# The taps of a depthwise convolution in another rhythm, with a later rank

## The chip, the cores and the metric

One NeuronCore of a Trainium2 chip runs the whole program. The metric is the device time of one execution in microseconds (us); less is better. Engines: TensorE (PE in the rows, its weight loads PEld), VectorE (DVE), ScalarE (ACT), GpSimd (POOL), and SyncE (SP), which issues the DMAs.

## What is computed

Two layers of a decoder trunk on 512 tokens of width 1024, in fp32. Each layer is a gated feed-forward half step, a token mixer, and a second feed-forward half step. The change lies in the mixer:

```python
def conv_module(u, conv_w, conv_b, ln_g, ln_b):
    u1, u2 = jnp.split(u, 2, axis=-1)
    u = u1 * jax.nn.sigmoid(u2)
    y = lax.conv_general_dilated(u, conv_w[:, None, :].astype(u.dtype), window_strides=(1,),
                                 padding=[(CONV_K - 1, 0)],
                                 dimension_numbers=('NWC', 'WIO', 'NWC'),
                                 feature_group_count=u.shape[-1]) + conv_b
    return jax.nn.silu(layernorm(y, ln_g, ln_b))

def token_mixer(...):
    proj = h @ w_in
...
    y_a = dilated_mixer(qa, ka, va, rel_bias[:, :HA]).reshape(b, s, A_W)
...
    ob = diff_attention(qb, kb, vb, lam, rel_bias[:, HA:])
    y_b = (rmsnorm(ob, subln_g) * (1.0 - lam_init)).reshape(b, s, B_W)
    y_c = conv_module(u, conv_w, conv_b, conv_ln_g, conv_ln_b)
    ys = jnp.einsum('gbsm,gmd->bsgd', jnp.stack([y_a, y_b, y_c]), w_branch)
    gates = jax.nn.sigmoid(h @ w_gate + b_gate).reshape(b, s, N_BRANCH, d)
    return jnp.sum(gates * ys, axis=2) @ w_out
```

The convolution has 31 taps and 512 channels, each channel for itself.

## The kernel before

Activations lie transposed, channels on partitions and the 512 tokens along the free dimension. Every fp32 weight and activation is split into a high and a low part (`halves`, lines 221 to 231: the high part by ScalarE in L226, the low part by VectorE in L230; `split`, L268 and L269, for activations), and each product is three matmuls (L274, L276, L278; in the projections L832, L834, L836). Weights come by DMA from SyncE into five raw buffers (`raw`, L218) and wait as split pairs in three.

The mixer (L1080) first makes the four channel tiles `u` of the convolution's input (`conv_in`, L719). Then it interleaves three streams that are written out by hand:

- the *filler*: the matmuls of the q, k, v projections for seven of eight heads' blocks (`project`, L816, 96 matmuls each; block 0 runs before), and then the first branch's gates (`gates`, L1074, 8 x 36 matmuls);
- the *attention* of eight blocks (`attention`, L908): four of the first kind (dilated, two heads each), four of the second (differential). It calls `pull(n)` between its own instructions, which emits n matmuls of the filler;
- the *convolution* (`conv`, L751): a generator. Each `yield n` asks to be called again n ticks later; `tick` (L1094) counts one for each pulled matmul and, beyond the attention, one for each matmul of the rest of the filler and of the second branch's gates.

One tap (L770; the first of each channel tile is L768) is a VectorE instruction over 128 x 512: `ca[j] = u * w + ca[j]`. There are 4 x 31 = 124 per layer. Before, the first 93 ask for 4 ticks each and the last 31 for 14. After the last tap comes the chain of the layer norm: sums over the channels by TensorE (`token_sum`, L322), broadcasts (`token_bcast`, L331), four subtractions (L787), squares, a reciprocal root, four products (L803), and four tiles of swish and split (L810, L811, L269). It asks for 127 ticks together. The four accumulators `ca` lie in two of the five raw weight buffers until the chain is through.

In ticks: 70 are pulled before the attention, the four blocks of the first kind pull 96 each (up to tick 454), the four of the second kind 108 each (up to 886), 18 follow, the filler ends at 960, and the second gates run to 1248. The third gates need the convolution's result and run after it, without ticks.

The order on each engine is fixed at build time: a scheduler gives each engine, whenever it takes it to be free, the ready instruction of the smallest rank. The rank is the order in which the program emits instructions. On the chip each engine then runs its list in that order. So a tap can run ahead of its place when its engine has nothing else that is ready, and a tap whose place has passed goes ahead of everything emitted later.

Other lines that are named below: L841 and L842 copy v out of the projection's PSUM banks and split it, L855 to L861 normalise q and k, L902 to L928 are the softmax, L937 transposes its result, L964 and L979 multiply it by v, L1058 to L1063 apply a gate.

Of the kernel before, what the change touches and what calls it, by code (L numbers as in the profile page):

```python
# [31 lines left out]
TAPS = 31  # L32
# [41 lines left out]
class Trunk:  # L74
# [676 lines left out]
    def conv(self, l):  # L751


        nc = self.nc

        ca = []
        for _ in range(2):
            t = self.raw()
            ca += [t[:, 0:T], t[:, T:2 * T]]


        prod = self.acc

        def tap(j, i):
            w = self.p(l, PO_CONVW + j * TAPS + i)
            u = self.up[j][:, i:i + T]
            if i == 0:
                nc.vector.tensor_scalar(ca[j], u, w, self.p(l, PO_CONVB + j), op0=ALU.mult, op1=ALU.add)  # L768
            else:
                nc.vector.scalar_tensor_tensor(ca[j], u, w, ca[j], op0=ALU.mult, op1=ALU.add)  # L770


        for j in range(4):
            for i in range(TAPS):
                tap(j, i)
                yield 4 if j < 3 else 14
        toks = range(4)
        nc.vector.tensor_tensor(prod, ca[2], ca[3], op=ALU.add)
        for j in range(2):
            nc.vector.tensor_tensor(prod, prod, ca[j], op=ALU.add)  # L780
        yield 1
        mean = self.token_sum([prod], toks, 1.0 / 512, 0.0)
        yield 16
        pb = self.token_bcast(mean, toks)
        yield 4
        for j in range(4):
            nc.vector.tensor_tensor(ca[j], ca[j], pb, op=ALU.subtract)  # L787
        yield 16
        for j in range(4):
            sq = self.t2k("sq")  # L790
            nc.scalar.activation(sq, ca[j], AF.Square)
            if j == 0:
                total = sq
            else:
                nc.vector.tensor_tensor(prod if j < 3 else total, total if j == 1 else prod, sq, op=ALU.add)
            yield 10
        v = self.token_sum([total], toks, 1.0 / 512, EPS)
        r = self.rsqrt(v, 4)
        yield 32
        pb = self.token_bcast(r, toks)  # L800
        yield 1
        for j in range(4):
            nc.vector.tensor_tensor(ca[j], ca[j], pb, op=ALU.mult)  # L803
        yield 17
        self.yc = []
        for j in range(4):
            g, b = self.p(l, PO_LNG + j), self.p(l, PO_LNB + j)
            sg = self.t2k("sg")
            nc.scalar.activation(sg, ca[j], AF.Sigmoid, bias=b, scale=g)
            nc.vector.tensor_scalar(ca[j], ca[j], g, b, op0=ALU.mult, op1=ALU.add)  # L810
            nc.vector.tensor_tensor(ca[j], ca[j], sg, op=ALU.mult)  # L811
            a = self.act_pair("yc")
            self.split(a, ca[j])
            self.yc.append(a)
# [265 lines left out]
    def mixer(self, l, stats, nxt):  # L1080
# [13 lines left out]
        def tick():  # L1094
            pull.count += 1
            if pull.count >= pull.due:
                pull.due = pull.count + next(conv, 1 << 30)
# [147 lines left out]
```

## Time and profile before

| | us |
|---|---|
| median of 3 runs | 2591.58 (2588.98 to 2593.63) |
| profiled execution | 2593.34 |
| its span | 2591.2 |
| TensorE busy | 2505.5 (97%) |
| VectorE busy | 1968.4 (76%) |
| ScalarE busy | 1124.6 (43%) |
| DMA queues, share of 16 engines | 37% |

Busy time is the time in which an engine has an instruction running. A matmul's end is modelled, so a busy TensorE need not be at its peak; the granted clock (PEclk, 1.00 is full speed, 2.4 GHz; 0.50 is 1.2 GHz) tells how fast it was allowed to run. Idle time of an engine is put down to the instruction whose end released the next one.

### The profile page before, as it was taken

How to read it: one execution, taken by the hardware profiler on the slowest of the kernel's cores; microseconds unless marked ns; L12 is line 12 of the kernel's file. 1: busy time of each engine (PE TensorE's matmuls, PEld its weight loads, DVE VectorE, ACT ScalarE, POOL GpSimd, SP SyncE). 2: the span in 40 equal slices, each digit the busy share in tenths (PEclk: the TensorE clock that was granted, in tenths of full speed). 3: DMA queues.
4: the chain of work that ended last, by engine and by line, in shares of the span. 5: the costliest groups of instructions: out<-in, count | busy, mean ns of one | idle time of the engine just before them, and what ended most of it. 6: DMA issues, size and time to landing. Idle time of an engine off the chain costs nothing.

```text
span 2591.2 us, 37974 instructions
## 1 busy us (share of the span) xinstructions
PE 2505.5 (97%) x15072; PEld 2201.5 (85%) x15072; DVE 1968.4 (76%) x3519; ACT 1124.6 (43%) x1765; POOL 30.5 (1%) x33
## 2 busy tenths in 40 slices
PE   6899999989999999999989999999899999999999
PEld 4889898877778889898989898898787778898988
DVE  8988876989873468979678796679898744785855
ACT  4435343545562345343455353435455523552533
POOL 2000000000000000000000000000000000000000
PEclk9999999989999999999999999999899999999999
DMA  7474644212223323737324553331122232233332
GB/s 264 163 244 158 236 149 127 80 46 76 78 90 98 90 74 98 260 107 260 107 65 157 209 183 123 96 88 54 50 81 78 90 94 93 66 106 98 101 97 89
DMA packets 97747, 312.20 MB, mean 120 GB/s; under 512 B 10345, under 2 KB 17257, under 8 KB 97570
## 3 DMA queue, kind: packets, MB, share of 16 engines
q1 hardware_dynamic: 97424, 309.65, 37.1%
q8 instruction: 118, 1.93, 0.3%
q14 instruction: 59, 0.48, 0.1%
q10 hardware_dynamic: 146, 0.14, 0.0%
HBM read 307.62 MB, written 6.06 MB: 121 GB/s over the span
## 4 chain that ended last, share of the span: by engine, by line
PE 82%; DVE 12%; ACT 3%; issue 2%; DMA 1%; SPq 0%; DVEq 0%; ACTq 0%
PE mm L583 16%; PE mm L274 13%; PE mm L276 13%; PE mm L278 13%; PE s L583 12%; PE mm L834 3%; PE mm L832 3%; PE mm L836 3%; DVE wr L770 2%; PE s L895 2%; DVE wl L230 2%; DVE ada L431 1%; DMA ada<-in_w_ada 1%; PE o L964 1%; DVE hx L491 1%
## 5 line engine op out<-in xcount | busy, mean ns | idle before, releaser
L226 ACT ACTIVATE wh<-wr 128x1024 fp32r<-128x1024 f32 (+1 forms) x481 | 485.2, 1010 | 641.6 <-PE mm L278 303.0
L230 DVE TENSOR_TENSOR wl<-wr,wh 128x1024 fp32r<-128x1024 f32 (+1 forms) x468 | 544.7, 1166 | 238.3 <-ACT wh L226 237.1
L274 PE MATMUL mm<-ah,wh 128*128 128x512 f32 (+1 forms) x752 | 287.1, 383 | 0.0
L274 PE MATMUL mm<-hh,wh 128*128 128x512 f32 (+1 forms) x776 | 281.6, 366 | 5.7 <-ACT wh L226 2.9
L278 PE MATMUL mm<-al,wh 128*128 128x512 f32 (+1 forms) x752 | 286.7, 382 | 0.0
L276 PE MATMUL mm<-hh,wl 128*128 128x512 f32 (+1 forms) x776 | 281.5, 366 | 5.2 <-DVE wl L230 5.2
L276 PE MATMUL mm<-ah,wl 128*128 128x512 f32 (+1 forms) x752 | 286.4, 382 | 0.0
L583 PE MATMUL mm<-sh,wh 128*128 128x256 f32 x936 | 268.4, 287 | 16.6 <-ACT wh L226 13.9
L278 PE MATMUL mm<-hl,wh 128*128 128x512 f32 (+1 forms) x776 | 276.5, 367 | 7.2 <-DVE hl L500 7.1
L583 PE MATMUL mm<-sh,wl 128*128 128x256 f32 x936 | 268.0, 286 | 0.5 <-DVE wl L230 0.5
L583 PE MATMUL mm<-sl,wh 128*128 128x256 f32 x936 | 267.7, 286 | 0.0
L509 DVE SCALAR_TENSOR_TENSOR x<-mm,res,x 128x512 f32<-128x512 f32 (+1 forms) x124 | 86.2, 697 | 156.2 <-PE mm L278 156.0
L583 PEld LDWEIGHTS mm<-sh,wh 128*128 128x128 f32 x936 | 182.1, 195 | 18.6 <-ACT wh L226 14.7
L834 PE MATMUL mm<-wl,hh 128*128 128x384 f32 x512 | 183.8, 359 | 8.5 <-DVE wl L230 8.5
L832 PE MATMUL mm<-wh,hh 128*128 128x384 f32 x512 | 177.3, 360 | 8.7 <-DVE v L842 8.7
L583 PEld LDWEIGHTS mm<-sh,wl 128*128 128x128 f32 x936 | 182.5, 195 | 1.2 <-DVE wl L230 0.8
L836 PE MATMUL mm<-wh,hl 128*128 128x384 f32 x512 | 183.5, 358 | 0.0
L583 PEld LDWEIGHTS mm<-sl,wh 128*128 128x128 f32 x936 | 182.6, 195 | 0.0
L770 DVE SCALAR_TENSOR_TENSOR wr<-u,par,wr 128x512 f32<-128x512 f32 x240 | 176.1, 744 | 0.2
L431 DVE SCALAR_TENSOR_TENSOR ada<-ada,cb 128x1024 f32<-128x1024 f32 x144 | 173.1, 1219 | 3.1 <-DMA ada<-in_w_ada 2.9
L274 PEld LDWEIGHTS mm<-hh,wh 128*128 128x128 f32 x776 | 147.6, 191 | 32.5 <-ACT hh L493 4.1
L583 PE MATMUL s<-hl,wh 128*128 128x256 f32 x624 | 175.1, 281 | 0.0
(218 smaller groups left out, 5603.8 us busy)
## 6 DMA issues: line engine op xcount, KB each, us to landing
wr<-in_w_up SPq DMA_DIRECT2D x156, 512.0 KB, 3.7
ada<-in_w_ada SPq DMA_DIRECT2D x144, 512.0 KB, 5.7
wr<-in_w_down SPq DMA_DIRECT2D x64, 512.0 KB, 5.4
wr<-in_w_qkv SPq DMA_DIRECT2D x64, 384.0 KB, 3.2
wr<-in_w_gate SPq DMA_DIRECT2D x48, 512.0 KB, 3.7
wr<-in_w_down SPq DMA_DIRECT2D x32, 384.0 KB, 3.1
wr<-in_w_branch SPq DMA_DIRECT2D x24, 512.0 KB, 3.6
wr<-in_w_u SPq DMA_DIRECT2D x16, 512.0 KB, 3.6
```

Source lines behind the costliest of these rows:

```text
L226: nc.scalar.activation(hi[:, :n], raw[:, :n], AF.Copy)
L230: eng.tensor_tensor(lo[:, :n], raw[:, :n], hi[:, :n].bitcast(F32), op=ALU.subtract)
L274: nc.tensor.matmul(ps[:, rng], w[0][:, wcol], ah[:, rng], start=start, stop=False)
L276: nc.tensor.matmul(ps[:, rng], w[1][:, wcol], ah[:, rng], start=False, stop=False)
L278: nc.tensor.matmul(ps[:, rng], w[0][:, wcol], al[:, rng], start=False, stop=stop)
L431: nc.vector.scalar_tensor_tensor(w, w, 1.0, cb, op0=ALU.mult, op1=ALU.mult, accum_out=self.mod[l][:, e:e + 1])
L509: self.nc.vector.scalar_tensor_tensor(self.x[d][:, rng], ps[:, rng], self.res[l][:, 8 * s + d:8 * s + d + 1], self.x[d][:, rng], op0=ALU.m ...
L583: nc.tensor.matmul(o, w[a][:, c], acts[k][b], start=first and (mi, k, x) == (0, 0, 0), stop=(k, x) == (3, 2), skip_group_check=True)
L770: nc.vector.scalar_tensor_tensor(ca[j], u, w, ca[j], op0=ALU.mult, op1=ALU.add)
L832: nc.tensor.matmul(o, hi[:, hs], w[0][:, ws], start=k == 0, stop=False)
L834: nc.tensor.matmul(o, hi[:, hs], w[1][:, ws], start=False, stop=False)
L836: nc.tensor.matmul(o, lo[:, hs], w[0][:, ws], start=False, stop=k == KD - 1)
```

## The change

Of each layer's 124 taps, the first 82 now ask for 5 and 6 ticks in turn, the next 24 for 18 each, and the last 18 for 8 each: 451, 432 and 144 ticks. In ticks, the three groups end at 451, 883 and 1027; before, the taps ended at 806. Each tap is also emitted with a rank 60 greater than its place (an offset of -60 in a block that otherwise makes ranks smaller), so 60 instructions emitted after it count as older. What follows the taps is as before.

```diff
-        for j in range(4):
-            for i in range(TAPS):
-                tap(j, i)
-                yield 4 if j < 3 else 14
+
+        for n in range(4 * TAPS):
+            with self.tc.high_priority(offset=-60):
+                tap(n // TAPS, n % TAPS)
+            yield 5 + n % 2 if n < 82 else 18 if n < 106 else 8
```

## Rows read from the trace of the kernel before

**Rows 1.** The page: busy time of two engines; granted clock in 40 slices.
```profile
PE 2505.5 (97%) x15072; PEld 2201.5 (85%) x15072; DVE 1968.4 (76%) x3519; ACT 1124.6 (43%) x1765; POOL 30.5 (1%) x33
...
PEclk9999999989999999999999999999899999999999
```

**Rows 2.** Windows, mixer: stretch, length, busy PE, PEld, DVE, ACT, POOL (instructions), clock, DMA.
```profile
476.00:614.00 138.00, 124.76 (x653) 102.73 (x653) 126.32 (x366) 66.88 (x183) 0.00 (x0) 0.94 0.18 52
...
614.00:767.00 153.00, 151.54 (x793) 121.09 (x792) 131.89 (x380) 88.62 (x171) 0.00 (x0) 1.00 0.26 79
767.00:834.00 67.00, 66.61 (x287) 52.99 (x286) 28.08 (x45) 20.76 (x25) 0.00 (x0) 1.00 0.35 109
...
1756.00:1896.00 140.00, 126.76 (x655) 104.69 (x656) 126.63 (x368) 67.12 (x183) 0.00 (x0) 0.93 0.18 53
...
476.00:520.00 44.00, 42.68 (x238) 35.12 (x237) 41.52 (x141) 25.49 (x70) 0.00 (x0) 1.00 0.19 60
...
614.00:680.00 66.00, 65.99 (x369) 55.62 (x368) 62.27 (x198) 34.24 (x83) 0.00 (x0) 1.00 0.31 92
```

**Rows 3.** Windows of TensorE alone: stretch, length, busy (instructions), clock, DMA.
```profile
544.00:546.00 2.00, 0.20 (x1) 0.56 0.47 91
546.00:554.00 8.00, 8.00 (x25) 0.50 0.25 94
...
568.00:572.00 4.00, 3.46 (x14) 0.57 0.34 98
```

**Rows 4.** Timeline of TensorE: start, duration, instruction, idle before it and its releaser.
```profile
568.54 0.69 PE L834 MATMUL mm<-wl,hh 128*128 128x384 f32 x1 [1.59 <-DVE wl L230]
...
587.69 0.42 PE L832 MATMUL mm<-wh,hh 128*128 128x384 f32 x1 [2.50 <-DVE v L842]
```

**Rows 5.** Timeline of VectorE before the last of these waits ended.
```profile
584.87 0.95 DVE L230 TENSOR_TENSOR wl<-wr,wh 128x768 fp32r<-128x768 f32 x1
585.74 0.74 DVE L770 SCALAR_TENSOR_TENSOR wr<-u,par,wr 128x512 f32<-128x512 f32 x1
586.40 0.28 DVE L841 CAST v<-mm 128x128 fp32r<-128x128 f32 x1
586.60 0.74 DVE L770 SCALAR_TENSOR_TENSOR wr<-u,par,wr 128x512 f32<-128x512 f32 x1
587.26 0.28 DVE L842 TENSOR_TENSOR v<-mm,v 128x128 fp32r<-128x128 f32 x1
```

**Rows 6.** Windows of line 832 alone: stretch, length, PE busy (count), PEld.
```profile
430.00:476.00 46.00, 20.51 (x61) 11.47 (x61) 1.00 0.31 90
476.00:520.00 44.00, 16.20 (x48) 8.97 (x48) 1.00 0.19 60
520.00:614.00 94.00, 26.39 (x77) 15.83 (x76) 0.91 0.17 49
```

**Rows 7.** Windows of line 770 (the taps) alone: stretch, length, DVE busy (count).
```profile
430.00:476.00 46.00, 21.86 (x31) 1.00 0.31 90
476.00:520.00 44.00, 13.39 (x18) 1.00 0.19 60
...
520.00:614.00 94.00, 34.17 (x46) 0.91 0.17 49
```

**Rows 8.** The page: DMA issues of gate weights.
```profile
wr<-in_w_gate SPq DMA_DIRECT2D x48, 512.0 KB, 3.7
```

**Rows 9.** Waits of TensorE, 476 to 614 us: total, times, longest.
```profile
PE mm L832 <- DVE v L842: 4.3, 2, 2.5
PE mm L834 <- DVE wl L230: 4.3, 4, 1.6
```

**Rows 10.** Timeline of VectorE: the first layer's last tap and pieces of the chain.
```profile
689.92 0.75 DVE L770 SCALAR_TENSOR_TENSOR wr<-u,par,wr 128x512 f32<-128x512 f32 x1
...
721.69 2.48 DVE L787 TENSOR_TENSOR wr<-wr,s 128x512 f32<-128x512 f32 x4 [0.89 <-PE s L331]
...
768.07 0.69 DVE L269 TENSOR_TENSOR ycl<-wr,ych 128x512 fp32r<-128x512 f32 x1 [0.30 <-ACT ych L268]
```

## The prediction

> **What bounds the kernel now.** I read the page first. TensorE is busy for 97% of the span and VectorE for 76%, and the granted clock is near full speed: of the 40 slices of 64.8 us only the ninth (from 518 us) and the 29th (from 1814 us) show a lower one, one in each layer's mixer [rows 1]. So most of the kernel is TensorE's own work, and a change of VectorE's order can win only where TensorE waits. All idle TensorE time together is 2591.2 - 2505.5 = 85.7 us.
>
> Then I cut the mixer of the first layer into stretches [rows 2]. The reader is to see that it changes its limit. In the 138 us of the first four heads (476 to 614) TensorE is busy for 124.8 us at a mean clock of 0.94 and VectorE for 126.3 us, 91.5%. In the second four (614 to 767) VectorE is at 86%, and TensorE idles 1.5 us. In the first stretch of gates beside which the change puts taps (767 to 834) VectorE is at 42%. The second layer repeats this (its row: 140 us, 126.8 us busy, clock 0.93).
>
> What the first heads lose is read off those rows. Idle: 138 - 124.8 = 13.2 us, and 13.2 us in the second layer. Low clock: at half speed half of the busy time is lost, so (1 - clock) x busy = 0.06 x 124.8 = 7.5 us, and 0.07 x 126.8 = 8.9 us. Together 20.7 and 22.1 us, **42.8 us in all**; the work without it is about 117 us per layer. The clock rows show how both hang together: TensorE, busy for 0.20 of the 2 us from 544 on, gets 0.56 there and then 0.50 until 554; the next low stretch (568 to 572) and one more near 590 follow an idle gap too [rows 3].
>
> Who holds TensorE up is seen in order of time [rows 4, 5]. The matmul at 587.69 us had waited 2.50 us for VectorE's L842, which frees a PSUM bank. VectorE in these microseconds does one small L841 or L842 (0.28 us), then a tap (0.74 us), then the next: two taps stand between the weight split at 584.87 and that L842. The gap that ends at 568.54 waited for a weight split.
>
> **Why taps stand there: they are overdue.** A tap's rank comes from the ticks, one per matmul of the filler. L832 is every third of these matmuls, and 96 belong to the first projection, which does not tick: ticks = 3 x count - 96. The cumulated L832 rows give 87 ticks at 476 us, 231 at 520, 462 at 614 [rows 6]. The taps done by then, with the first tap of each channel tile (L768: two of the four before 476, two after 520) are 33, 51 and 99 [rows 7]. Due, at one per 4 ticks up to 93 and one per 14 beyond, were 22, 58 and 99. So the taps began 11 ahead, as fill of idle time, but by 520 us they are 7 behind and at 614 just level: then a tap is the oldest ready work and is issued ahead of newer softmax, split and copy instructions. From 520 to 614 there are 46 (34.2 us of 94).
>
> **The change part by part.** Nothing is added or removed: 124 taps per layer of 0.74 us (0.67 us from start to start in [rows 5]), the same chain behind them, no DMA issued or moved. Only ranks move, on VectorE's queue alone.
>
> (a) *First heads.* Due are now one tap per 5.5 ticks, and 60 ranks later. About 1200 TensorE, VectorE and ScalarE instructions stand in the stretch [rows 2] for 375 ticks, 3.2 per tick, so 60 ranks are some 19 ticks or 3.4 taps. Due at the three points: 12, 39, 81, against 33, 51, 99 that were done. The head start of 33 stays (VectorE was full of taps before 476 because nothing else was ready), so a tap is hardly ever overdue and should only fill what is left. Of 66 taps some 30 to 48 remain here. VectorE's need: 126.3 - 66 x 0.67 = 82 us other work, plus at most 48 x 0.67 = 32, is 114 us, just under TensorE's 117. I take TensorE as the limit, with a residue: a tap that has begun still delays what comes ready behind it by up to 0.74 us. The nearest row with taps as fill is 476 to 520, 18 taps, where TensorE idled 1.32 of 44 us, 3% [rows 2]: 3.5 us per layer. Of the three low-clock stretches I leave one: a third of 7.5 and 8.9, 2.5 and 3.0 us. Gain 20.7 - 6.0 = 14.7 and 22.1 - 6.5 = 15.6: **30.3 us**. Bounds: all 42.8, or little (first rival).
>
> In the Trainium skill, "TensorE: Matmul & The Clock Gate" (Part 1) calls the slow clock the default, which activity lifts; by that rule a TensorE that is no longer held up keeps the full clock, the two sums of 2.5 and 3.0 us fall away too, and the gain would be 5.5 us larger. The row of that stretch agrees (clock 1.00 [rows 2]); I keep the third because some gaps will be longer.
>
> (b) *Second heads.* 25 taps stood here. By the end of these heads 106 are due, less the 63 to 81 done by then: 25 to 43, at most 29 us where 17 stood, on a VectorE with 21 us free, while the normalisation chain of the convolution moves out to the gates. The row 614 to 680 has 18 taps in 66 us, VectorE at 94%, and TensorE idle for 0.01 us [rows 2]. Cost between 0 and 3 us per layer; I take 1, **+2 us**.
>
> (c) *Gates.* 18 taps (12 us) and the chain (some 18 us of VectorE work, worked out below) beside gates where VectorE has 39 us free. Nothing, as long as the third gates get their input in time. The two raw weight tiles that the convolution holds are held some 40 us longer, so weights run through three buffers instead of five beside the second gates. Twelve loads fall in 67 us, one per 5.6 us, each lands in 3.7 us [rows 8]; the second heads ran on three buffers too. Cost 0; if that cover failed, each late weight would cost at most its 3.7 us of transfer.
>
> **The sum** against the profiled run (2593.3 us; span 2591.2): 2593.3 - 30.3 + 2 = 2565.0. That run lies 1.8 us above the median shown, so against the median of 2591.6 it is **2563 us**, 1.1% less. What a measurement can tell from no change is 0.2%, 5.2 us.
>
> **Rivals.**
> *Fill is as bad as overdue* (0.15). Several taps of [rows 5] lie between an L841 and its L842, where VectorE's next instruction was a moment from ready; a later rank does not forbid that, and the 31 taps before 476 us [rows 7] were put in as fill too. Then the waits on L842 and on weight splits, 4.3 us each [rows 9], and the clock stay: 16.1 of 20.7 us. Gain 4.6 and about 5.5 us: 2582 us. Against it: 476 to 520 with such fill lost 1.3 us.
> *TensorE's work is the end anyway* (0.10). With 97% against 76%, shifting VectorE's work changes no total; if stalls only move to the second heads or the gates, the time is that of before, 2586 to 2597. The same follows if the ranks alter little because fill had run ahead of them. Against it: 7 taps overdue.
> The Trainium skill, "Perfetto Trace Analysis" (Identifying the Most-Contended Engine), wants the engine of highest occupancy optimised first; by the whole span that is TensorE and this change is worth nothing. The row of the first heads disagrees for that stretch, 91.5% VectorE against 90.4% TensorE.
> *The chain comes late* (0.08), the slower side. Place: the third gates, whose first product with the convolution falls 24 matmuls after 834 us, at 839.6. The last tap is due at tick 1022, plus 60 ranks; beside gates (357 instructions for 288 ticks [rows 2]) these are 48 ticks. Tick 960 is the start of the second gates, 767; each tick lasts 67/288 = 0.233 us; so a last tap that waits for its rank runs at 767 + 110 x 0.233 = 792.6. From last tap to the last split the chain took 769 - 690 = 79 us before [rows 10]. Then 871 against 839.6: 32 us idle per layer, less the 15 gained, is +17, twice: 2625 us. It decides when the chain takes over 47 us there. Against it: its VectorE work is 18 us (26 instructions over 128 x 512 at some 0.62, as the four subtractions in 2.48 [rows 10], and 2 us of small ones); it took 79 us beside heads whose instructions went first, and beside gates VectorE is mostly free, so that the taps also run ahead of their rank.
>
> **How the numbers follow.** The forecast, most of the 42.8 us gone, has 0.67 and spans 2549 (all of it) to 2578 (half of the 30). With the first rival and the near part of the second the range is 2547 to 2587; what lies above it is about 0.17, below 0.03. Faster takes 0.67 and nearly all of the first rival: 0.80; the same, 0.11; slower, the late chain and a rest of stalls elsewhere, 0.09.
>
> **What the changed profile would show.** Right: in the first heads TensorE idle near 4 us and at most one low-clock stretch, fewer than 20 taps after the halfway point of where 46 stood, taps running through the second heads into the gates, that part of the mixer some 15 us shorter per layer, all else equal. Wrong: taps between L841 and L842 with TensorE waiting as before (first rival); idle time reappearing in the second heads (second); a wait of TensorE on a split of the convolution's output in the third gates (third).

## The result, and the profile after

The changed kernel takes **2555.29 us** (median of 4, 2552.69 to 2558.10) against 2592.28 us (2588.98 to 2593.63): ratio **0.986 [0.9842, 0.9876]**, 37 us less. The prediction was 2563 us, 2547 to 2587. The profiled execution took 2555.3 us with a span of 2553.2, so 38.0 us less span than before. Code lines behind the taps have moved down by one: L833, L835, L837 are the projections (L832 to L836 before), L842 and L843 the copies of v, L896 the scores, L903 the softmax.

The page, busy time and granted clock in 40 slices:

```profile
PE 2486.7 (97%) x15072; PEld 2192.3 (86%) x15072; DVE 1965.9 (77%) x3519; ACT 1123.4 (44%) x1765; POOL 30.6 (1%) x33
...
PEclk9999999999999999999999999999999999999999
```

The same instructions as in [rows 1] and nearly the same VectorE time (1968.4 to 1965.9 us), but TensorE is busy for 18.8 us less, and the two slices with a lower clock are gone. The share of TensorE, 97%, has not moved: it told nothing of this change.

Windows of the mixers, with columns as in [rows 2]: first heads of layer 0 (they now end at 597 us, not 614), of layer 1, then the second heads and the gates of layer 0:

```profile
476.00:597.00 121.00, 118.82 (x657) 99.29 (x658) 110.83 (x343) 66.96 (x182) 0.00 (x0) 0.97 0.21 60
...
1738.70:1858.70 120.00, 117.20 (x655) 97.80 (x655) 110.78 (x343) 66.92 (x182) 0.00 (x0) 0.99 0.20 59
...
597.00:746.00 149.00, 146.33 (x760) 117.52 (x759) 133.72 (x371) 83.04 (x160) 0.00 (x0) 1.00 0.28 84
...
767.00:834.00 67.00, 67.00 (x298) 54.12 (x297) 37.79 (x63) 24.04 (x32) 0.00 (x0) 1.00 0.33 103
```

The first heads run the same 655 matmuls or so in 121 and 120 us where they took 138 and 140. TensorE idles 2.2 and 2.8 us there (13.2 before), at a clock of 0.97 and 0.99. Windows of the taps alone (line 770, so without the first tap of each channel tile), as in [rows 7]:

```profile
476.00:520.00 44.00, 8.80 (x12) 1.00 0.26 76
476.00:597.00 121.00, 31.09 (x42) 0.97 0.21 60
597.00:772.00 175.00, 35.05 (x47) 1.00 0.28 84
```

The first heads hold 42 taps, where 18 + 46 = 64 were [rows 7]; the second heads hold 47, where 25 were; no tap runs beside the gates. The last one starts at 709.5 us.

What TensorE still waits for in these 121 us (engine, line, releaser: us in total, times, longest):

```profile
PE s L896 <- DVE m L903: 0.9, 1, 0.9
PE s L938 <- DVE m L903: 0.5, 1, 0.5
PE mm L835 <- DVE wl L230: 0.3, 1, 0.3
PE s L896 <- DVE pT L269: 0.2, 1, 0.2
```

The waits on v and on weight splits, 4.3 us each in [rows 9], are 0 and 0.3. One stretch at half clock is left in these heads. Timeline of TensorE, then windows of TensorE alone:

```profile
572.69 0.33 PE L938 MATMUL s<-ident,p 128*128 128x128 f32 x1 [0.51 <-DVE m L903]
573.93 0.85 PE L896 MATMUL s<-qT,qT 64*128 64x384 f32 x3 [0.91 <-DVE m L903]
...
574.00:576.00 2.00, 1.76 (x6) 0.63 0.00 0
576.00:578.00 2.00, 1.67 (x7) 0.50 0.30 23
578.00:580.00 2.00, 2.00 (x8) 0.50 0.48 174
```

And VectorE at that moment:

```profile
572.21 0.41 DVE L903 CUSTOM_DVE_ANT_0 p<-s,G 128x256 f32<-128x256 f32 x1
...
572.71 0.74 DVE L770 SCALAR_TENSOR_TENSOR wr<-u,par,wr 128x512 f32<-128x512 f32 x1
...
573.45 0.41 DVE L903 CUSTOM_DVE_ANT_0 p<-s,G 128x256 f32<-128x256 f32 x1
...
573.88 0.74 DVE L770 SCALAR_TENSOR_TENSOR wr<-u,par,wr 128x512 f32<-128x512 f32 x1
```

Between the two softmax steps stands a tap, and TensorE waits for the second step. It is the picture of [rows 5], now before a wait of 0.91 us where that one was 2.50 [rows 4].

**Where the 38.0 us of span came from.** I cut the whole span into short windows and summed two things: idle time, and busy time x (1 - clock). Idle TensorE fell from 85.7 to 66.5 us (-19.2), the loss to the low clock from 30.0 to 17.8 (-12.2), and TensorE's busy time taken at full clock from 2475.5 to 2468.9 (-6.6). Outside the heads and the gates beside which the ticks run, neither idle time (55.6, then 55.5) nor clock loss (13.1, then 13.0) changed.

### The profile page after: what moved, and what is told of

Its sections match the earlier page's. It is cut to its first block, busy times and chain, and to the rows that moved or that the text cites. A ratio compares the mean times of both kernels' runs of the same rounds, so it can differ in the third digit from the quotient of the medians.

```text
span 2553.2 us, 37958 instructions
## 1 busy us (share of the span) xinstructions
PE 2486.7 (97%) x15072; PEld 2192.3 (86%) x15072; DVE 1965.9 (77%) x3519; ACT 1123.4 (44%) x1765; POOL 30.6 (1%) x33
## 4 chain that ended last, share of the span: by engine, by line
PE 81%; DVE 12%; ACT 3%; DMA 2%; issue 2%; POOL 0%; DVEq 0%; SPq 0%; ACTq 0%
PE mm L583 15%; PE mm L274 14%; PE mm L276 14%; PE mm L278 14%; PE s L583 11%; PE mm L837 3%; PE mm L835 3%; PE mm L833 3%; DVE wl L230 2%; PE s L896 2%; DVE wr L770 1%; DMA wr<-in_w_up 1%; PE o L965 1%; PE s L938 1%; DVE ada L431 1%
## 5 line engine op out<-in xcount | busy, mean ns | idle before, releaser
L835 PE MATMUL mm<-wl,hh 128*128 128x384 f32 x512 | 179.7, 351 | 1.3 <-DVE wl L230 1.2
L837 PE MATMUL mm<-wh,hl 128*128 128x384 f32 x512 | 180.6, 353 | 0.0
L833 PE MATMUL mm<-wh,hh 128*128 128x384 f32 x512 | 175.3, 347 | 1.8 <-DVE v L843 1.8
L583 PE MATMUL s<-hh,wl 128*128 128x256 f32 x624 | 174.1, 279 | 1.2 <-DVE wl L230 1.2
```

What stands on the lines that cost most here:

```text
L583: nc.tensor.matmul(o, w[a][:, c], acts[k][b], start=first and (mi, k, x) == (0, 0, 0), stop=(k, x) == (3, 2), skip_group_check=True)
L833: nc.tensor.matmul(o, hi[:, hs], w[0][:, ws], start=k == 0, stop=False)
L835: nc.tensor.matmul(o, hi[:, hs], w[1][:, ws], start=False, stop=False)
L837: nc.tensor.matmul(o, lo[:, hs], w[0][:, ws], start=False, stop=k == KD - 1)
```

## The experiments

The expectations name the theories by a letter. **O**: order; a tap whose place has passed stands ahead of newer work. **L**: load; what matters is how many taps the first heads hold. **R**: the later rank does it. **Q**: backlog; due taps and VectorE's own work together exceed a stretch, and a tap that only fills costs little. **C**: moving the chain of the layer norm out of the second heads does it. Diffs are against the loop of the changed kernel.

**1. The rhythm alone, and the rank alone.**

```diff
# e1_rhythm
-            with self.tc.high_priority(offset=-60):
-                tap(n // TAPS, n % TAPS)
+            tap(n // TAPS, n % TAPS)
# e2_rank
-            yield 5 + n % 2 if n < 82 else 18 if n < 106 else 8
+            yield 4 if n < 93 else 14
# e4_early
-            with self.tc.high_priority(offset=-60):
+            with self.tc.high_priority(offset=60):
```

> The new rhythm alone (5 and 6, 18, 8 ticks), each tap at the rank of its place. Theory O (order: TensorE loses time where overdue taps stand ahead of newer instructions): due at 231 and 462 ticks are 42 and 84 taps, against some 45 that fill had done by the first point; overdue only late in the first heads: 2556 to 2568 us. Theory L (load: the number of taps in the first heads, times 0.67 us, sets their length): 84 - 33 = 51 taps instead of 48, 4 us more than the changed kernel over two layers: 2559. Theory R (the rank does it, the rhythm is nothing): 2585 to 2592.

> The rank alone: 4 and 14 ticks as before, each tap 60 ranks later. Theory O: due at 231 ticks is (231 - 19)/4 = 53 where before 51 were done, so hardly a tap is overdue any more: 2560 to 2575 us. Theory L: by the end of the first heads 98 taps are due as before, 65 of them in the first heads: 2586 to 2592. Theory R: all of the gain, 2553 to 2560.

> The new rhythm with the rank 60 earlier than its place instead of 60 later. Theory O: due at 231 and 462 ticks are 45 and 87, so taps go ahead of the work of some 19 ticks for most of the first heads: 2568 to 2582 us. Theory L: 87 - 33 = 54 taps there instead of 48, 8 us more than the changed kernel over two layers: 2563. Theory R: as slow as before or slower, 2590 to 2600.

Measured: rhythm alone 2554.72 us, 0.9866 [0.9852, 0.9881]; rank alone 2576.50 us, 0.9955 [0.9939, 0.9972]; new rhythm with a rank 60 *earlier* 2555.87 us, 0.9867 [0.9851, 0.9884]. All the gain is the rhythm's. Beside it the rank, 60 either way, is worth nothing that can be measured; beside the old rhythm it is worth about a third of the gain, 12.6 us against the 2589.05 us of before that was measured beside it. R falls as the cause. Two of the three results lie in no theory's range: the rank alone falls between O (to 2575) and L (from 2586), and the earlier rank is 7 us below L's 2563. Windows of the rank alone, same stretch as above, and its waits there:

```profile
476.00:597.00 121.00, 109.32 (x580) 91.11 (x579) 114.37 (x341) 59.83 (x163) 0.00 (x0) 0.93 0.18 54
...
PE s L896 <- DVE m L903: 4.1, 2, 2.6
PE mm L833 <- DVE v L843: 2.5, 1, 2.5
PE s L938 <- DVE p L925: 1.6, 2, 1.2
PE mm L835 <- DVE wl L230: 1.5, 4, 0.9
```

580 matmuls against 657 in the same time. The rank did take the taps from between v's two halves (4.3 us [rows 9], now 2.5), but the lack of VectorE time came out elsewhere, at the softmax, 4.1 us. A later rank chooses who waits; it makes hardly any room (two taps fewer in the first heads). Why these heads are still 5.4 and 6.3 us shorter than before is open.

**2. No taps at all.** Each tile's first tap is computed and the other 30 are left out; ticks and chain as before.

```diff
# e3_notaps
-            with self.tc.high_priority(offset=-60):
+            if n % TAPS == 0:
                 tap(n // TAPS, n % TAPS)
-            yield 5 + n % 2 if n < 82 else 18 if n < 106 else 8
+            yield 4 if n < 93 else 14
```

> The kernel before without 30 of the 31 taps of each channel tile (left out: 120 taps per layer, so the convolution has one tap); ticks and chain as before. The floor of what taps can cost: by the rows of before, 16.8 us of low clock and 26.4 us of idle time stand in the first heads and 2.9 us of idle time in the second. Theories O and L alike: all of it goes, 2545 to 2550 us. If tighter matmul sequences add what the busy time of the changed kernel shows (6.7 us), 2538 to 2543. If much below 2538, taps cost TensorE beyond its waits.

Measured: 2540.49 us, 0.9813 [0.9799, 0.9828], 5 us below what idle time and clock alone promised. I take this as the floor for any order of the taps: they cost 49 to 52 us before (2589.05 or 2592.28 less 2540.49) and 15 us after, though they are 248 x 0.67 = 166 us of VectorE work in either. Windows of first and second heads:

```profile
476.00:586.00 110.00, 109.87 (x631) 91.27 (x630) 88.25 (x305) 65.21 (x179) 0.00 (x0) 1.00 0.24 71
586.00:746.00 160.00, 159.88 (x833) 127.93 (x833) 121.75 (x360) 92.75 (x176) 0.00 (x0) 1.00 0.25 81
```

The first heads take 110.8 us without taps. VectorE's own work there is 88 us, so 22 us are free: 33 taps at 0.67 us.

**3. How the taps are spread within the first heads.** Both put 82 taps into the first 460 ticks or fewer, as the change does, and have no rank offset: one crowds them at the front (as many due at 520 us as before the change), one at the back.

```diff
-            with self.tc.high_priority(offset=-60):
-                tap(n // TAPS, n % TAPS)
-            yield 5 + n % 2 if n < 82 else 18 if n < 106 else 8
+            tap(n // TAPS, n % TAPS)
# e9_front
+            yield 4 if n < 60 else 10 if n < 82 else 18 if n < 106 else 8
# e10_back
+            yield 7 if n < 40 else 4 if n < 82 else 18 if n < 106 else 8
```

> The new number of taps in the first heads, put early: 4 ticks for 60 taps, 10 for 22, then 18 and 8 as in the change; no rank offset. At 231 ticks 58 are due as before (overdue against fill), at 462 ticks 82 as in the change. Theory L (the number of taps in the first heads against what VectorE has room for): as the rhythm alone, 2552 to 2559 us. Theory O (overdue taps stand in the way): the stretch around 520 us loses what it lost before, the rest does not: 2564 to 2576.

> The same number put late: 7 ticks for 40 taps, 4 for 42, then 18 and 8; no rank offset. At 231 ticks 33 are due (fill is far ahead), at 462 ticks 85. Theory L: as the rhythm alone, 2552 to 2561 us. Theory O: nothing overdue before some 350 ticks, then crowded: 2554 to 2568. If early and late differ by over 10 us the order within the stretch counts.

Measured: front 2555.01 us, 0.9864 [0.9849, 0.9878]; back 2564.21 us, 0.9901 [0.9884, 0.9917]. With taps 7 behind at 520 us as before, the front version loses nothing against e1_rhythm. Being late at that point was not the harm; what came after it was. That fits L and not O. The back version fits O's range and lies 3 us above L's: it has first heads of the same length (121.5 us), and pays in the second heads, 153 us where e1_rhythm has 148 (149 and 147). Why these lose 5 us per layer was not followed further than that TensorE idles 1.3 us more there and loses 1.7 and 3.4 us to the clock.

**4. Taps as fill.** The rank 600 later, with the old rhythm and with the new one; 600 ranks are some 190 ticks by the prediction's 3.2 per tick.

```diff
# e5_fill
-            with self.tc.high_priority(offset=-60):
+            with self.tc.high_priority(offset=-600):
...
-            yield 5 + n % 2 if n < 82 else 18 if n < 106 else 8
+            yield 4 if n < 93 else 14
# e11_new_fill
-            with self.tc.high_priority(offset=-60):
+            with self.tc.high_priority(offset=-600):
```

> The old rhythm (4 and 14 ticks) with a rank 600 later: some 190 ticks, so no tap is overdue in the first heads and taps there are fill alone. Theory L: fill stops where VectorE is full, 40 to 46 taps in the first heads, 2550 to 2560 us. Theory O: the same range. If the rhythm in ticks mattered by itself: above 2570.

> The change with its rank 600 later instead of 60. Theory Q (backlog: TensorE loses time where taps that are due, with VectorE's own work, exceed the stretch; taps that only fill cost little): nothing is due in the first heads, 30 fill taps as with the old rhythm and this rank, 111 us without loss; in the second heads 48 taps are due at their start where 63 are done, 96 at their end, so no backlog there either: 2546 to 2554 us, at or below the change. If fill in the second heads costs as it did with the old rhythm and this rank (15 us per layer): 2565.

Measured: old rhythm 2565.66 us, 0.9909 [0.9894, 0.9924]; new rhythm **2546.87 us**, 0.983 [0.9815, 0.9844]. Each of its four runs (2545.75 to 2547.87) is below each of the changed kernel's (2552.69 to 2558.10), and it is 6 us from the floor. It beats both kernels. The old rhythm missed both theories' range by 6 us. Windows of e5_fill, then of e11_new_fill: first heads, second heads.

```profile
476.00:588.00 112.00, 111.79 (x640) 93.73 (x639) 104.24 (x332) 65.10 (x181) 0.00 (x0) 1.00 0.23 67
588.00:746.00 158.00, 146.65 (x774) 119.31 (x773) 146.80 (x405) 83.27 (x164) 0.00 (x0) 0.98 0.21 68
```

```profile
476.00:588.00 112.00, 111.79 (x640) 93.71 (x640) 104.17 (x332) 65.22 (x181) 0.00 (x0) 1.00 0.23 67
588.00:746.00 158.00, 155.59 (x789) 123.68 (x789) 142.14 (x386) 85.93 (x164) 0.00 (x0) 0.98 0.24 78
```

In both, the first heads hold 30 taps and TensorE idles 0.2 us in 112: fill is free, as long as it fits into the 33. Then 59 and 60 taps are left for the second heads. At one per 4 ticks they come due faster than they are done: counted as in the prediction, 86 are due at 610 us where 73 are done (in e11_new_fill 64 and 70). TensorE idles 11.4 us in this window, 2.7 of them in one wait of the norm's chain, which stands there too; at the new rhythm, with the chain beside the gates, 2.4.

**5. The slow middle, and the chain.** First the change without its slow middle: the last 42 taps at 8 ticks each. Then the same with the chain held back by 240 ticks, about to where the change has it. And before's loop with the chain alone moved there.

```diff
# e6_ends_early
-            yield 5 + n % 2 if n < 82 else 18 if n < 106 else 8
+            yield 5 + n % 2 if n < 82 else 8
# e13_early_chain_late
-            yield 5 + n % 2 if n < 82 else 18 if n < 106 else 8
+            yield 5 + n % 2 if n < 82 else 8
+        yield 240
# e12_chain_late
-            with self.tc.high_priority(offset=-60):
-                tap(n // TAPS, n % TAPS)
-            yield 5 + n % 2 if n < 82 else 18 if n < 106 else 8
+            tap(n // TAPS, n % TAPS)
+            yield 4 if n < 93 else 14
+        yield 221
```

> The change with its last 42 taps at 8 ticks each: the same first heads, but the taps end at tick 787 and the chain of the norm stands beside the second heads, as before, instead of beside gates. If the first heads are all of the gain: 2553 to 2558 us. If moving the chain and the last taps out to the gates is part of it (VectorE in the second heads then needs 115 us of its own, 42 x 0.67 = 28 for taps, 143 of 150 in all, chain included): 2559 to 2575.

> The change with its last 42 taps at 8 ticks, which lost the gain, and the chain moved out to the gates again by 240 more ticks. Theory Q: the loss came from taps due at one per 8 ticks between 610 and 690 us, before the chain began at 714: 2572 to 2588 us. Theory C (chain: the chain of the norm beside the second heads took the room that the taps need): 2553 to 2560.

> The old rhythm and rank, and only the chain moved: 221 more ticks before its first step, so that it stands beside the second gates as in the change. Theory Q: the first heads keep their 66 due taps and their loss, the second heads lost 1.5 us: 2583 to 2592 us. If the chain in the second heads was what cost the time: 2560 or less.

Measured: no slow middle 2587.36 us, 0.9983 [0.9974, 0.9992]; with the late chain 2580.19 us, 0.9965 [0.9955, 0.9976]; the late chain alone 2591.37 us, 1.0003 [0.9993, 1.0012]. The first result says most: it lies 12 us above the slower range that was expected. Its first heads are those of the change (120.7 and 120.0 us, 42 taps), and still nearly all of the gain is gone, in the second heads: 174.7 and 168.7 us where the change has 150.3 and 148.4 (some 5 us of TensorE's work stands there and no longer beside the gates; with the late chain it is moved back, and the second heads still take 165.9 and 160.8). The chain explains 7 us of the 32, and alone it is worth nothing: C falls as the main cause. The rest is the taps. Windows of e6_ends_early, a stretch of the second heads; then those of the change; then of e11_new_fill, all engines and the taps alone:

```profile
610.00:690.00 80.00, 70.56 (x365) 58.53 (x364) 76.40 (x226) 36.61 (x78) 0.00 (x0) 0.93 0.24 74
```

```profile
610.00:690.00 80.00, 78.29 (x425) 63.94 (x423) 78.25 (x240) 45.47 (x94) 0.00 (x0) 1.00 0.29 86
```

```profile
610.00:690.00 80.00, 79.94 (x424) 64.78 (x424) 77.17 (x221) 46.84 (x90) 0.00 (x0) 1.00 0.24 78
...
610.00:690.00 80.00, 24.70 (x34) 1.00 0.24 78
```

VectorE is nearly as busy in e6_ends_early as in the change, but TensorE has run 60 matmuls fewer. The taps in these 80 us are 34 against 27, and e11_new_fill has 34 there too, with 79.94 us of TensorE. So here the count is not the cause. It is whether the taps are due: counted as in the prediction, e6_ends_early has 88, 96 and 107 due at 610, 630 and 657 us and 84, 93 and 104 done, e11_new_fill 64, 78 and 86 due and 70, 78 and 87 done. Tap by tap, 7 of the 48 that run after 597 us (with the first of a channel tile) run ahead of their place in e6_ends_early, 29 of 48 in the change. One of the long waits of e6_ends_early, on the timelines of VectorE and TensorE:

```profile
656.89 0.75 DVE L770 SCALAR_TENSOR_TENSOR wr<-u,par,wr 128x512 f32<-128x512 f32 x1
657.56 0.61 DVE L929 SCALAR_TENSOR_TENSOR p<-p,rd,p 128x384 f32<-128x384 f32 x1
658.09 0.16 DVE L921 RECIPROCAL rd<-den 128x2 f32<-128x2 f32 x1
658.16 1.20 DVE L230 TENSOR_TENSOR wl<-wr,wh 128x1024 fp32r<-128x1024 f32 x1
659.28 0.15 DVE L927 TENSOR_TENSOR rd<-rd,neglam 128x1 f32<-128x1 f32 x1
659.35 0.74 DVE L770 SCALAR_TENSOR_TENSOR wr<-u,par,wr 128x512 f32<-128x512 f32 x1
660.01 0.48 DVE L928 TENSOR_SCALAR p<-p,rd 128x512 f32<-128x512 f32 x1
660.41 0.28 DVE L842 CAST v<-mm 128x128 fp32r<-128x128 f32 x1
660.61 0.74 DVE L929 SCALAR_TENSOR_TENSOR p<-p,rd,p 128x512 f32<-128x512 f32 x1
...
661.41 0.90 PE L938 MATMUL s<-ident,p 128*128 128x128 f32 x3 [2.40 <-DVE p L929]
```

Reciprocal, its product with -lambda, scaling and combination (L921, L927, L928, L929) are steps of one softmax, each needing the one before. A due tap stands between the second and the third, and another ahead of the chain: 1.3 of the 2.40 us for which TensorE waits at its end. That due taps in this stretch do it, and fill does not, is what the three kernels side by side show; not every microsecond of the 21.6 that these second heads lose to idle time and clock is followed to a tap like this.

**6. A later end.** The last 18 taps at 16 ticks, which puts the chain behind the second gates.

```diff
# e7_late
-            yield 5 + n % 2 if n < 82 else 18 if n < 106 else 8
+            yield 5 + n % 2 if n < 82 else 18 if n < 106 else 16
```

> The change with its last 18 taps at 16 ticks instead of 8: by fill the taps end as before, but the chain's places move from tick 1027 to 1171, and its second half stands behind the second gates. Then TensorE waits before the third gates for sums, root, broadcast, products and splits, some 14 us less the 5.6 us of matmuls that need none of it: 8 us per layer, 2565 to 2575 us. If the chain ran as soon as its data are there, whatever its place: 2553 to 2558.

Measured: 2559.33 us, 0.988 [0.9866, 0.9895], 6 us below the expected range. The intervals of this and of the change overlap. The taps have not moved at all (42 and 47, the last at 710.4 us), since they run as fill ahead of their place; only the chain has, its last split to 827.78 us. TensorE did not wait for it: between 790 and 870 us its one wait is 0.9 us on a weight split.

## Why the prediction was right, point by point

The time lay in the range, 8 us under the point. But part of the gain came from a term that the sum did not have, and one reason was only half right.

**The limit by stretch: right.** The gain is all in the mixers, on a TensorE that was "97% busy" all along.

**(a) First heads, gain 14.7 and 15.6 us: nearly right.** By idle time and clock loss summed as above (first heads from first to last product): before 13.2 + 7.5 and 13.2 + 9.4 us, after 2.2 + 3.1 and 2.8 + 1.7. That is 15.4 and 18.1. The residue was put at 3.5 us idle and 2.5 to 3.0 of clock; one low stretch per layer was left, as forecast. Wait and clock hang together in one direction: no run lost clock in the first heads where TensorE did not idle there (e5_fill, e11_new_fill), but e9_front idled 4.1 us and lost none. How much is lost is partly luck: e4_early idles 6.2 us in the first heads of either layer and loses 4.7 us to the clock in one and nothing in the other. The Trainium skill, "TensorE: Matmul & The Clock Gate" (Part 1), calls the slow clock the default, which activity lifts; e11_new_fill, which idles 0.2 us, agrees (clock 1.00). In the change, still held up a little, the prediction's reading of it, that no clock loss is left, would have promised 4.8 us too much.

**The reason, "taps stand there because they are overdue": the step that failed in part.** For before it holds by the prediction's own count: 7 behind at 520 us, and 10 behind at 560 (84 due, 74 done). But being 7 behind is not yet a loss: e9_front is as far behind at 520 us, is back to 3 at 560 (71, 68), and loses nothing against e1_rhythm. And in the change a tap was to be "hardly ever overdue" and only to fill. That did not come: after 520 us, the halfway point in ticks, there are 30 taps, not fewer than 20, and they are not fill (by 597 us 79 to 83 are due, 76 are done). What counts is how many fall due before the first heads end, against 33 that fit. The table shows it for layer 0; due is reckoned at tick 454, 3.2 ranks to a tick, less the 33 done before 476 us; both counts have the first taps of the channel tiles (L768) in them, which the rows of line 770 leave out:

| | due | run | length us | idle + clock us |
|---|---|---|---|---|
| e3_notaps | - | 2 | 110.8 | 0.1 |
| e11_new_fill | 15 | 31 | 111.1 | 0.2 |
| e5_fill | 33 | 31 | 110.9 | 0.2 |
| the change | 46 | 43 | 120.6 | 5.3 |
| e1_rhythm | 49 | 47 | 122.3 | 9.1 |
| e9_front | 48 | 48 | 121.6 | 4.1 |
| e10_back | 49 | 46 | 121.5 | 5.6 |
| e4_early | 50 | 51 | 126.7 | 10.9 |
| e2_rank | 64 | 64 | 132.0 | 18.8 |
| before | 66 | 66 | 137.4 | 20.8 |

From 31 to 66 taps the stretch grows by 26.5 us, 0.76 us for each, which is a tap and some clock. So in the main it is load (L) in the first heads: the taps that fall due there. Past the room, due and run rise together in every run, so the two were not separated there; 31 taps as fill cost nothing, and more than that were not tried. Nor does the count explain all: e2_rank has two taps fewer than before and is 5.4 us shorter, and e4_early takes 122.5 us in layer 1 with the same taps. The 60 ranks, on which the prediction leaned with 19 ticks, are within this a matter of 3 taps, and e1_rhythm against the change shows them to be worth nothing beside the new rhythm. Each edit also shifts the build-time order of the other engines a little; what that is worth by itself was not tested.

**TensorE's work, "about 117 us": mis-sized.** Without taps the stretch takes 110.7 us of TensorE (e3_notaps). But not all of the difference is false work: 633 matmuls start there in e3_notaps and 646 before, as filler runs further ahead while the heads wait, and 646 at the mean of e3_notaps would be 113 us. So some 4 us of what the windows call busy in the first heads before is not work. Matmul ends are modelled and overlap the next start, so a matmul that comes a little late still looks joined; that reading was argued, not tested. Over the span, with the same 15072 matmuls, such busy time shrank by 6.6 us, most of the 9.7 us between the sum of 2565.0 and the profiled 2555.3. It does not follow the taps alone: it is 2463 us in e1_rhythm and 2470 in e3_notaps. The cause stays open.

**(b) Second heads, +1 us per layer: right by its size, and not by its reason.** Idle time there went from 1.46 to 2.67 us, +1.2, and the same in layer 1. Room alone did not bring that: e6_ends_early has the same 47 taps there and loses 21.6 us. The price stayed at 1 because the middle asks for a tap only every 18 ticks, so that most of the 47 are fill (by the count above, 29 against 7). The prediction took the slow middle for granted.

**(c) Gates at nothing: right.** Their idle time is 0.6 and 0.2 us (0.4 and 0.3 before). The sum was 2565.0 against a profiled 2555.3: -33.5 for (a) where -30.3 was put, +2.4 for (b), and -6.6 that was not in it.

**The rivals.** *Fill is as bad as overdue* fell: 30 taps as fill in the first heads cost 0.2 us (e11_new_fill). *TensorE's work is the end anyway* fell with the 37 us. The Trainium skill, "Perfetto Trace Analysis" (Identifying the Most-Contended Engine), wants the engine of highest occupancy optimised first. Over the whole span that is TensorE, and yet the 37 us came from the order of VectorE's work, which was the busier of the two in the first heads (91.5% against 90.4%). *The chain comes late* did not come, by a wide margin. (Its last tap is due at tick 1019, not 1022, which is 0.7 us.) In the change the chain follows its ticks, as its sums wait for TensorE:

```profile
758.37 0.16 DVE L325 TENSOR_SCALAR ts<-s 128x4 f32<-128x4 f32 x1 [2.48 <-PE s L322]
...
786.38 2.48 DVE L804 TENSOR_TENSOR wr<-wr,s 128x512 f32<-128x512 f32 x4 [2.54 <-PE s L331]
...
796.55 0.68 DVE L269 TENSOR_TENSOR ycl<-wr,ych 128x512 fp32r<-128x512 f32 x1
...
815.77 0.39 PE L274 MATMUL mm<-ych,wh 128*128 128x512 f32 x1
```

From the mean's row to the end of the last split it takes 39 us, and it is done 18.5 us before the first product that reads it. Even 31 us later (e7_late) TensorE does not wait for it.

## What to carry to other kernels

Work that nobody waits for is best spread by room: for each stretch, take the busy engine's free time without it (leave it out once and look), divide by the length of one piece, and let no more than that fall *due* there; what runs beyond it as fill cost 0.2 us here. Giving such work a late place cost nothing here (e11_new_fill), while a crowd of due pieces lengthens the short dependent chains on its engine, at whose ends others wait. Judge an engine by stretch, and do not take TensorE's busy time for its work: a run without the suspect shows how short the stretch can be.

## What was not expected of the hardware

- TensorE's busy time is not work. In the first heads 646 matmuls, at full clock, were 116.6 us busy before, and 649 were 113.2 in e1_rhythm. Over the span the same 15072 were 2475.5 and 2463.4.
- A late VectorE reached TensorE by way of ScalarE. The longest wait in the second heads of e6_ends_early is for a weight split that stands in ScalarE's order behind a softmax step, for which it had idled 3.03 us, and a gate; each of these needed a table load of 1.28 us. Timelines of ScalarE and TensorE there:

```profile
681.91 1.28 ACT L905 ACT_TABLE_LOAD   x1 [3.03 <-DVE rs L296]
683.20 0.40 ACT L905 ACTIVATE p<-p,m 128x128 f32<-128x128 f32 x1
...
684.10 1.28 ACT L1059 ACT_TABLE_LOAD   x1
685.40 0.69 ACT L1059 ACTIVATE z<-mm,par 128x512 f32<-128x512 f32 x1
685.98 1.99 ACT L226 ACTIVATE wh<-wr 128x1024 fp32r<-128x1024 f32 x2
...
687.08 0.49 PE L274 MATMUL mm<-hh,wh 128*128 128x512 f32 x1 [2.92 <-ACT wh L226]
```

- Taps that are nominally to run beside the gates all ran by 709.5 us: in this kernel their place in ticks bounds only how late they run, while the chain behind them, which needs TensorE, keeps its place.
